# GpSimd for the context's elementwise work, dense copies of the scanned states, tables kept and re-read, and stores on another queue

## The chip, the core and the metric

One core of a Trainium2 chip runs the whole step of a hybrid S5 and pooling backbone in float32. The metric is the device time of one execution in microseconds (us); three executions of the kernel before took 2468.7, 2470.66 and 2472.08, the median is 2470.66.

## The reference, cut to what matters

A context of 128 tokens and a latent grid of 1024 tokens go through two layers. Layer 0 mixes with an S5 scan in both directions, layer 1 with pooling; each has a LayerNorm, a SwiGLU and another LayerNorm. The change lies in layer 0: the S5 mixer's output, its GLU, and the context's LayerNorm and SwiGLU.

```python
def s5_mixer(h, ..., h0_re, h0_im):
    u = h.reshape(bsz, seq_len, SSM_GROUPS, SSM_GROUP)
    y = u * d_skip
    for d in range(N_DIRS):
        s_re, s_im, f_re, f_im = s5_scan(u, ab_re, ab_im, bb_re, bb_im, h0_re[:, d], h0_im[:, d], reverse=(d == 1))
        y = y + einsum('blgp,ghp->blgh', s_re, c_re[d]) - einsum('blgp,ghp->blgh', s_im, c_im[d])
    v = gelu(y.reshape(bsz, seq_len, D_MODEL)) @ glu_w + glu_b
    val, gate = split(v, 2)
    return val * sigmoid(gate), ...

xc = layer_norm(DEEPNORM_ALPHA * xc + g1c * oc, ln_g[i, 0], ln_b[i, 0])
fc = swiglu(modulate(xc, sh2c, sc2c), ffn_w_gate[i], ffn_w_up[i], ffn_w_down[i])
xc = layer_norm(DEEPNORM_ALPHA * xc + g2c * fc, ln_g[i, 1], ln_b[i, 1])
```

`xl`, the latents, goes the same way with its own gates.

## The kernel before

Channels lie on partitions, 8 blocks (`kt`) of 128. For the scan, eight tokens in a row form a chunk: the latents have 128 chunks, the context 16. The work until the latents' GLU runs through these stages:

- *Tables.* `ssm_params`, then per block `ssm_u`, `ssm_in`, `ssm_tables`: the inputs u and the tables of each block are made. Output tables go to memory as `mo` (1 MB a block, stores `mo<-otab`) and `kd` (the part inside a chunk, read back as `mk`, 0.5 MB). Beside it the weights of the ada modulation are read, tile by tile (`adaw<-ada_w`, 0.5 MB), and used (`ada_steps`, L148). After the first bank 32 tiles remain: in the kernel before 16 of them are asked for by `self.step(fill, 2)` in this loop and 16 in the loop over the context's y.
- *Context's scan and y.* `ssm_scan_ctx` runs 15 steps; a step is six VectorE instructions (L477, L482) on the state buffers `Z` of both directions, which are 128 partitions x 145 chunks x 64 floats, so that the same state of the next chunk lies 64 floats on. `ssm_y_ctx` loads `mk` and `mo` of a block and multiplies (L620, L623), applies Gelu, transposes (L634).
- *Context's GLU, LayerNorm, SwiGLU up* (`ctx0a`, `ctx0b`: L815 with names glu and ffn) while the latents are scanned (`ssm_scan_lat`, 127 steps). All their elementwise work is on VectorE, in one queue with the scan.
- *Latents' y* (`ssm_y`, L649 and L652). `stack` first swaps halves of Z so that one product covers both real and imaginary parts; the products then read Z with its stride of 64 floats. Each block's result goes to memory (`yd`, eight stores on SP) and is read again by `yr<-yd` on GpSimd's queue.
- After that the latents' GLU begins (`glu` for A and B), with the rest of the context's SwiGLU as filling, and then the remaining layers.

Instructions of an engine run in program order; DMAs of a queue are issued in order. The scheduler of the tile framework decides the order on each engine from the code's order and its own timeline. Buffers decide when a load may start: `raw` has three (weights of 0.5 MB), `mk` and `mo` two each. In the orders below `Z_562` is the forward state buffer and `Z_566` the backward one; `mo_86` to `mo_93`, `kd_94` to `kd_101` and `yd_102` to `yd_109` are blocks 0 to 7.

Of the kernel before, what the change touches and what calls it, by code (L numbers as in the profile page):

```python
# [20 lines left out]
KT = 8  # L21
# [20 lines left out]
class Kernel:  # L42
# [540 lines left out]
    def load_mo(self, tmp, kt):  # L583

        m = tmp.tile([128, 8, 128], F32, tag="mk", name="mk", bufs=2)
        kd = self.kd[kt]
        for s in range(8):
            self.nc.sync.dma_start(m[16 * s:16 * s + 16], kd.rearrange("g h m -> h g m")[:, :, 16 * s:16 * s + 128])
        mo = tmp.tile([128, 2048], F32, tag="mo", name="mo", bufs=2)
        self.nc.sync.dma_start(mo, self.mo[kt])  # L590
        return m, mo.rearrange("p (d x g m) -> p d x g m", d=2, x=2, g=4)

    def stack(self, tmp, kt, c0, n, tag):


        nc = self.nc
        for d in range(2):
            z = self.Z[d][:, c0 + d:c0 + d + n, :].rearrange("p c (r g) -> p r g c", r=2)[:, :, 4 * kt:4 * kt + 4]
            t = tmp.tile([64, 4, n], F32, tag=tag, name=tag, bufs=2)
            if d == 0:  # L600
                cp = lambda o, i: nc.scalar.activation(o, i, AF.Copy)
            else:
                cp = lambda o, i: nc.vector.tensor_copy(o, i)
            cp(t, z[64:128, 0])
            cp(z[64:128, 0], z[0:64, 1])
            cp(z[0:64, 1], t)

    def ssm_y_ctx(self, tmp, kt):
# [29 lines left out]
    def ssm_y(self, tmp, kt):  # L638

        nc = self.nc  # L640
        m, ot = self.load_mo(tmp, kt)
        self.stack(tmp, kt, 0, NCL, "swl")
        y = tmp.tile([128, 8, NCL], F32, tag="yl", name="yl", bufs=2)
        py = [self.psum(f"py{x}") for x in range(2)]
        for gp in range(4):
# [4 lines left out]
            for x in range(2):  # L650
                for d in range(2):
                    nc.tensor.matmul(o[x], ot[:, d, x, gp, :], self.Z[d][:, d:d + NCL, 32 * x + 4 * kt + gp],  # L652
                                     start=False, stop=(d == 1))
# [3 lines left out]
        for t in range(8):  # L657
            nc.sync.dma_start(yd[t], y[16 * t:16 * t + 16])

# [3 lines left out]
    def ssm(self):  # L663
# [19 lines left out]
        with R("ssu") as tmp:  # L683
            for kt in range(KT):
                self.ssm_u(tmp, kt)
                if kt == 0:
                    self.ssm_u_ctx(tmp)
                self.step(fill, 2)
                self.ssm_powers(kt)
# [13 lines left out]
        with R("ssy") as tmp:  # L703
            self.adp = tmp
            self.yb = [tmp.tile([128, 8, 8, 16], F32, tag="yl", name=f"yb{q}", bufs=2) for q in range(2)]
            for q in range(2):
                self.nc.gpsimd.memset(self.yb[q], 0.0)
            for kt in range(KT):
                self.ssm_y_ctx(tmp, kt)
                self.step(fill, 2)  # L710
            self.step(fill, 2)
            self.ctx0a()
            self.ssm_scan_lat()
            self.adp = self.rawc = None
            for kt in range(KT):
                self.ssm_y(tmp, kt)
# [104 lines left out]
    def pair(self, b, w, x, name):  # L821
# [8 lines left out]
        return p1, p2  # L830

    def glu(self, b, x, fill=iter(()), vx=lambda a: a, vs=lambda a: a):
        nc, I = self.nc, self.I
        gw = I["ssm_glu_w"][0].rearrange("(k p) m -> p k m", p=128)
        for m in range(8):
# [3 lines left out]
            nc.scalar.activation(sg, pg, AF.Sigmoid, bias=self.glu_b[:, 1, m:m + 1])  # L839
            nc.vector.scalar_tensor_tensor(sg, pv, self.glu_b[:, 0, m:m + 1], sg, op0=OP.add, op1=OP.mult)  # L840
            nc.vector.scalar_tensor_tensor(vx(b.x[:, m, :]), vs(sg), self.gate[0, 0][:, b.i, m:m + 1],
                                           vx(b.x[:, m, :]), op0=OP.mult, op1=OP.add)
            next(fill, None)
# [57 lines left out]
    def ln_stats(self, b):  # L901

        nc = self.nc
        v = nc.vector
        n = b.n
# [24 lines left out]
        v.scalar_tensor_tensor(q, q, -0.5, r, op0=OP.mult, op1=OP.mult)  # L930
        v.scalar_tensor_tensor(r, q, 1.5, r, op0=OP.add, op1=OP.mult)
        for q in range(4):
# [160 lines left out]
    def build(self):  # L1093
        tc, nc = self.tc, self.nc
        with ExitStack() as st:
# [15 lines left out]
            self.XC = P("xcres").tile([128, 8, 128], F32, name="XC")  # L1111
            self.gate, self.lnm = {}, {}
            self.ident = self.cp.tile([128, 128], F32, name="ident")
            make_identity(nc, self.ident)
            self.ssm()
            fill = self.ctx0b()
            self.step(fill, 15)
            self.whl = P("whl")
            xr = P("xres")
# [140 lines left out]
```

## Time and profile before

| | us |
|---|---|
| median of three executions | 2470.66 |
| the profiled execution | 2463.38 |
| its span | 2461.6 |

| engine | busy us | share of the span |
|---|---|---|
| TensorE matmul (PE) | 2269.7 | 92% |
| TensorE weight load (PEld) | 1896.8 | 77% |
| VectorE (DVE) | 1267.1 | 51% |
| ScalarE (ACT) | 921.4 | 37% |
| GpSimd (POOL) | 168.2 | 7% |

The shares are means over the whole span. The change touches the first 515 us, so the rows below are of single stretches there. A row of instructions names the line, the engine, the operation, output<-inputs, shapes and count; busy time of a stretch is summed over an engine's instructions; PEclk is the granted clock of TensorE as a share of full speed, DMA share the mean busy share of the core's 16 DMA engines. "[x <-y]" is idle time of the engine ahead of the row and what ended it. SPq and POOLq rows are DMA issues. The trace has two records for each float32 matrix product with 128x128 operands. Matmul records overlap, so their pace is read from the starts, not from the durations.

### The profile page before, as it was taken

The numbers are of one execution on the slowest core, as the hardware profiler recorded it, in microseconds if no ns is written. First come the engines' busy times: TensorE is split into PE (matmuls) and PEld (weight loads), VectorE is DVE, ScalarE is ACT, GpSimd is POOL, SyncE is SP. The second block draws the span as 40 slices with busy tenths as digits, with TensorE's granted clock in tenths as the row PEclk, the third lists the DMA queues.
The fourth block names the chain that finished last, engine by engine and source line by source line (L and its number), as shares of the span: only waits on it lengthen the run. The fifth ranks groups of instructions, "written<-read, shape, count | busy, mean of one in ns | idle before, by whom it ended". The sixth has DMA issues, their size and how long they took to land.

```text
span 2461.6 us, 33280 instructions
## 1 busy us (share of the span) xinstructions
PE 2269.7 (92%) x13105; PEld 1896.8 (77%) x13105; DVE 1267.1 (51%) x2478; ACT 921.4 (37%) x1359; POOL 168.2 (7%) x182
## 2 busy tenths in 40 slices
PE   4877777689999999999999999889999999999997
PEld 2655677678887777788888888777788888888996
DVE  6789672053537222456422675778422455422476
ACT  3763126163216222443322453325322443322364
POOL 4920000000001000100000010002000100000000
PEclk7986898899999999999999999999999999999998
DMA  7759766684555554533333234865333223333453
GB/s 223 243 154 269 214 189 150 170 261 124 150 162 175 159 159 158 189 107 95 94 99 98 95 99 142 242 189 151 94 95 102 94 95 97 99 96 94 146 197 103
DMA packets 470076, 361.42 MB, mean 147 GB/s; under 512 B 15504, under 2 KB 418720, under 8 KB 467616
## 3 DMA queue, kind: packets, MB, share of 16 engines
q1 hardware_dynamic: 466032, 349.30, 48.0%
q10 hardware_dynamic: 2736, 5.80, 0.6%
q0 software_dynamic: 1152, 4.19, 0.5%
q8 instruction: 103, 1.69, 0.3%
q14 instruction: 53, 0.43, 0.1%
HBM read 340.77 MB, written 18.35 MB: 146 GB/s over the span
## 4 chain that ended last, share of the span: by engine, by line
PE 78%; DMA 12%; DVE 4%; ACT 3%; SPq 1%; POOL 1%; issue 1%; ACTq 0%; DVEq 0%; POOLq 0%
PE ffn L811 13%; PE ffn L813 13%; PE ffn L812 13%; PE dn L812 6%; PE dn L811 6%; PE dn L813 6%; PE ffn L815 3%; PE dn L815 3%; DMA adaw<-ada_w 3%; PE glu L811 2%; PE glu L813 2%; PE glu L812 2%; DMA raw<-ffn_w_up 2%; PE py L652 2%; DMA raw<-ffn_w_down 1%; DMA mo<-mo 1%
## 5 line engine op out<-in xcount | busy, mean ns | idle before, releaser
L795 ACT ACTIVATE wh<-raw 128x1024 fp32r<-128x1024 f32 (+1 forms) x326 | 341.7, 1049 | 944.0 <-PE ffn L812 613.9
L796 DVE TENSOR_TENSOR wl<-raw,wh 128x1024 fp32r<-128x1024 f32 (+1 forms) x326 | 394.6, 1211 | 496.0 <-ACT wh L795 489.0
L812 PE MATMUL dn<-hkl,wh 128*128 128x512 f32 (+1 forms) x880 | 304.5, 348 | 0.3 <-DVE hkl L796 0.3
L813 PE MATMUL dn<-hkh,wl 128*128 128x512 f32 (+1 forms) x880 | 303.0, 347 | 0.0
L811 PE MATMUL ffn<-xp,wh 128*128 128x512 f32 x704 | 275.9, 392 | 2.2 <-ACT wh L795 2.2
L813 PE MATMUL ffn<-xp,wl 128*128 128x512 f32 x704 | 276.1, 392 | 0.5 <-DVE wl L796 0.5
L811 PE MATMUL ffn<-xm,wh 128*128 128x512 f32 x704 | 274.4, 391 | 1.3 <-ACT xm L795 0.7
L812 PE MATMUL ffn<-xp,wh 128*128 128x512 f32 x704 | 275.4, 391 | 0.0
L813 PE MATMUL ffn<-xm,wl 128*128 128x512 f32 x704 | 274.9, 391 | 0.0
L812 PE MATMUL ffn<-xm,wh 128*128 128x512 f32 x704 | 274.8, 390 | 0.0
L811 PE MATMUL dn<-hkh,wh 128*128 128x512 f32 (+1 forms) x880 | 262.5, 348 | 0.9 <-ACT hkh L795 0.9
L856 DVE TENSOR_TENSOR h<-ffn,sg 128x512 f32<-128x512 f32 x88 | 60.6, 689 | 248.9 <-PE ffn L813 248.2
L812 PEld LDWEIGHTS dn<-hkl,wh 128*128 128x128 f32 x880 | 166.6, 189 | 21.0 <-DVE hkl L796 0.5
L813 PEld LDWEIGHTS dn<-hkh,wl 128*128 128x128 f32 x880 | 166.5, 189 | 20.5
L811 PEld LDWEIGHTS dn<-hkh,wh 128*128 128x128 f32 x880 | 163.3, 189 | 23.4 <-ACT hkh L795 1.7
L815 PE MATMUL ffn<-xmc,raw 128*128 128x128 f32 x1184 | 148.1, 282 | 30.3 <-DMA raw<-ffn_w_up 12.3
L815 PEld LDWEIGHTS ffn<-xmc,raw 128*128 128x128 f32 x1184 | 141.0, 195 | 40.2 <-DMA raw<-ffn_w_up 16.4
L811 PEld LDWEIGHTS ffn<-xm,wh 128*128 128x128 f32 x704 | 132.1, 188 | 33.2 <-issue 3.8
L811 PEld LDWEIGHTS ffn<-xp,wh 128*128 128x128 f32 x704 | 133.1, 189 | 31.0 <-ACT wh L795 2.5
L813 PEld LDWEIGHTS ffn<-xp,wl 128*128 128x128 f32 x704 | 132.8, 189 | 28.9 <-DVE wl L796 1.0
L812 PEld LDWEIGHTS ffn<-xp,wh 128*128 128x128 f32 x704 | 132.8, 189 | 28.5 <-issue 0.7
L813 PEld LDWEIGHTS ffn<-xm,wl 128*128 128x128 f32 x704 | 132.2, 188 | 29.0 <-issue 1.5
(313 smaller groups left out, 3238.6 us busy)
## 6 DMA issues: line engine op xcount, KB each, us to landing
raw<-ffn_w_down SPq DMA_DIRECT2D x126, 512.0 KB
raw<-ffn_w_gate SPq DMA_DIRECT2D x125, 512.0 KB
raw<-ffn_w_up SPq DMA_DIRECT2D x125, 512.0 KB
adaw<-ada_w SPq DMA_DIRECT2D x96, 512.0 KB
raw<-ssm_glu_w SPq DMA_DIRECT2D x48, 512.0 KB
mo<-mo SPq DMA_DIRECT2D x16, 1024.0 KB
rc<-ffn_w_down SPq DMA_DIRECT2D x40, 256.0 KB
mo<-otab SPq DMA_DIRECT2D x32, 256.0 KB
```

The source lines that it names most:

```text
L652: nc.tensor.matmul(o[x], ot[:, d, x, gp, :], self.Z[d][:, d:d + NCL, 32 * x + 4 * kt + gp], start=False, stop=(d == 1))
L795: nc.scalar.activation(h, src, AF.Copy)
L796: nc.vector.tensor_tensor(l, src, h.bitcast(F32), op=OP.subtract)
L811: nc.tensor.matmul(ps, wh, xh, start=start, stop=False)
L812: nc.tensor.matmul(ps, wh, xl, start=False, stop=False)
L813: nc.tensor.matmul(ps, wl, xh, start=False, stop=stop)
L815: nc.tensor.matmul(ps, w[0], x[0], start=start, stop=stop)
L856: nc.vector.tensor_tensor(h[:, f, :], pu, sg, op=OP.mult)
```

## The change

Five things change.

1. Ada's weight tiles are asked for earlier: three per block from block 3 on in the table loop, three ahead of the context's y, one in each of its blocks.
2. `load_mo` keeps what is loaded: four `mk` and two `mo` buffers, and the latents' blocks go in the order 6, 7, 4, 5, 0, 1, 2, 3, so that blocks 6 and 7 need no load and 4 and 5 only `mo`.
3. For the latents `stack` is replaced by `stack_dense`: a copy of the block's states with chunks next to each other (three buffers), on ScalarE, VectorE and GpSimd; the products read the copy. For the context `stack`'s copies of the second direction move from VectorE to GpSimd.
4. While `scanning` holds, the context's elementwise work (GLU, LayerNorm, the first six blocks of SwiGLU) goes to GpSimd. ScalarE copies from PSUM what GpSimd needs, and an instruction with two operations becomes two. The reciprocal stays on VectorE.
5. The eight stores of a block's y are issued by GpSimd instead of SP.

```diff
     def load_mo(self, tmp, kt):
-        m = tmp.tile([128, 8, 128], F32, tag="mk", name="mk", bufs=2)
-        kd = self.kd[kt]
-        for s in range(8):
-            self.nc.sync.dma_start(m[16 * s:16 * s + 16], kd.rearrange("g h m -> h g m")[:, :, 16 * s:16 * s + 128])
-        mo = tmp.tile([128, 2048], F32, tag="mo", name="mo", bufs=2)
-        self.nc.sync.dma_start(mo, self.mo[kt])
-        return m, mo.rearrange("p (d x g m) -> p d x g m", d=2, x=2, g=4)
+        if kt not in self.mks[-4:]:
+            m = tmp.tile([128, 8, 128], F32, tag="mk", name="mk", bufs=4)
+            for s in range(8):
+                self.nc.sync.dma_start(m[16 * s:16 * s + 16],
+                                       self.kd[kt].rearrange("g h m -> h g m")[:, :, 16 * s:16 * s + 128])
+            self.mks.append(kt)
+            self.held["m", kt] = m
+        if kt not in self.mos[-2:]:
+            mo = tmp.tile([128, 2048], F32, tag="mo", name="mo", bufs=2)
+            self.nc.sync.dma_start(mo, self.mo[kt])
+            self.mos.append(kt)
+            self.held["o", kt] = mo
...
     def stack(self, tmp, kt, c0, n, tag):
...
-                cp = lambda o, i: nc.vector.tensor_copy(o, i)
+                cp = lambda o, i: nc.gpsimd.tensor_copy(o, i)
...
+    def stack_dense(self, tmp, kt, d):
+        nc = self.nc
+        z = self.Z[d][:, d:d + NCL, :].rearrange("p c (r g) -> p r g c", r=2)[:, :, 4 * kt:4 * kt + 4]
+        sd = tmp.tile([128, 2, 4, NCL], F32, tag="sd", name="sd", bufs=3)
+        for x in range(2):
+            for r in range(2):
+                o, i = sd[64 * r:64 * r + 64, x], z[64 * x:64 * x + 64, r]
+                if d == 0 and x == 0:
+                    nc.scalar.activation(o, i, AF.Copy)
+                elif x == 1 and r == 0:
+                    nc.gpsimd.tensor_copy(o, i)
+                else:
+                    nc.vector.tensor_copy(o, i)
+        return sd
...
     def ssm_y(self, tmp, kt):
-        self.stack(tmp, kt, 0, NCL, "swl")
+        sd = [self.stack_dense(tmp, kt, d) for d in range(2)]
...
-                    nc.tensor.matmul(o[x], ot[:, d, x, gp, :], self.Z[d][:, d:d + NCL, 32 * x + 4 * kt + gp],
+                    nc.tensor.matmul(o[x], ot[:, d, x, gp, :], sd[d][:, x, gp, :],
...
-            nc.sync.dma_start(yd[t], y[16 * t:16 * t + 16])
+            nc.gpsimd.dma_start(yd[t], y[16 * t:16 * t + 16])
...
     def ssm(self):
-                self.step(fill, 2)
+                self.step(fill, 2 if kt < 3 else 3)
...
+            self.scanning = True
+            self.step(fill, 3)
             for kt in range(KT):
                 self.ssm_y_ctx(tmp, kt)
-                self.step(fill, 2)
-            self.step(fill, 2)
+                self.step(fill, 1)
+            self.drain(fill)
             self.ctx0a()
             self.ssm_scan_lat()
-            for kt in range(KT):
+            for kt in (6, 7, 4, 5, 0, 1, 2, 3):
                 self.ssm_y(tmp, kt)
...
+    def elem(self, b, early=True):
+        return self.nc.gpsimd if self.scanning and early and not b.split else self.nc.vector
+
+    def in_sb(self, b, v, ps):
+        if v is self.nc.vector:
+            return ps
+        t = b.tmp.tile([128, b.n], F32, tag="lq" + b.tg, name="cp", bufs=1)
+        self.nc.scalar.activation(t, ps, AF.Copy)
+        return t
+
+    def stt(self, b, out, x, s, y, op0, op1, bias=None):
+        v = self.elem(b)
+        if v is self.nc.vector:
+            v.scalar_tensor_tensor(out, x, s, y, op0=op0, op1=op1)
+            return
+        t = b.tmp.tile([128, 2, b.n], F32, tag="lt" + b.tg, name="st", bufs=3)[:, 0]
...
+        if bias is not None:
+            self.nc.scalar.activation(t, x, AF.Identity, bias=bias)
+        else:
+            v.tensor_scalar(t, x, s, None, op0=op0)
+        v.tensor_tensor(out, t, y, op=op1)
...
     def ffn_up(self, b, l, x, h, first=None):
-            nc.vector.tensor_tensor(h[:, f, :], pu, sg, op=OP.mult)
+            v = self.elem(b, f < 6)
+            v.tensor_tensor(h[:, f, :], self.in_sb(b, v, pu), sg, op=OP.mult)
...
     def ln_stats(self, b):
-        v = nc.vector
+        v = self.elem(b)
...
-        pm = self.ones_mm(b, t[:, 0], "lnm")
+        pm = self.in_sb(b, v, self.ones_mm(b, t[:, 0], "lnm"))
...
-        v.reciprocal(r, q)
-        v.scalar_tensor_tensor(q, pv, LN_EPS / (ALPHA * ALPHA), r, op0=OP.add, op1=OP.mult)
+        nc.vector.reciprocal(r, q)
+        self.stt(b, q, pv, LN_EPS / (ALPHA * ALPHA), r, OP.add, OP.mult, self.epsc[:, 0:1])
```

The two instructions of `glu` and the two that follow in `ln_stats` go through `stt` in the same way; in `build`, `self.scanning = False` follows `self.step(fill, 15)`.

On TensorE, where the latents' y begins, the order before was this (glu and ffn are the context's products, lnm and lnv its LayerNorm sums, py the latents' y):

```order
L815 MATMUL glu<-xmc,raw 128x128 x88
L898 MATMUL lnm<-lt,ones 128x128
L898 MATMUL lnv<-sq,ones 128x128
L815 MATMUL ffn<-xmc,raw 128x128 x192
L652 MATMUL py_3938<-Z_562,mo 128x128
L815 MATMUL ffn<-xmc,raw 128x128 x8
L652 MATMUL py_3938<-Z_566,mo 128x128
L652 MATMUL py_3939<-Z_562,mo 128x128
```

Now it is this:

```order
L841 MATMUL glu<-xmc,raw 128x128 x104
L952 MATMUL lnm<-lt,ones 128x128
L952 MATMUL lnv<-sq,ones 128x128
L841 MATMUL ffn<-xmc,raw 128x128 x135
L677 MATMUL py_3969<-sd,mo 128x128
L841 MATMUL ffn<-xmc,raw 128x128
L677 MATMUL py_3970<-sd,mo 128x128
L841 MATMUL ffn<-xmc,raw 128x128 x16
L677 MATMUL py_3969<-sd,mo 128x128
```

135 of the context's 240 SwiGLU products of this part stand ahead of the first y product instead of 192; 105 stand between y products.

On SP's queue at the same place, where the tables of the third and fourth block of y are asked for, the order before was this:

```order
L588 DMA mk<-kd_96 16x8x128 x5
L658 DMA yd_102<-yl 16x8x128 x8
L588 DMA mk<-kd_96 16x8x128 x2
L658 DMA yd_103<-yl 16x8x128 x8
L588 DMA mk<-kd_96 16x8x128
L590 DMA mo<-mo_88 128x2048
L588 DMA mk<-kd_97 16x8x128 x8
L590 DMA mo<-mo_89 128x2048
```

Now it is this:

```order
L589 DMA mk<-kd_94 16x8x128 x2
L595 DMA mo<-mo_90 128x2048
L589 DMA mk<-kd_94 16x8x128 x6
L830 DMA raw<-ffn_w_gate 128x8x128
L589 DMA mk<-kd_95 16x8x128 x2
L595 DMA mo<-mo_91 128x2048
L589 DMA mk<-kd_95 16x8x128 x6
L830 DMA raw<-ffn_w_up 128x8x128
```

No store of y stands between loads any more.

On GpSimd's queue the context's work is followed by copies (sd) and the stores of y, which did not stand there before:

```order
L988 TENSOR_TENSOR XC<-XC,lr 128x256 x4
L1003 TENSOR_SCALAR xmc<-XC,lnm_2900 128x128 x8
L910 TENSOR_TENSOR hc<-cp,sg 128x128 x6
L628 COPY sd<-Z_562 64x512
L628 COPY sd<-Z_566 64x512
L628 COPY sd<-Z_562 64x512
L628 COPY sd<-Z_566 64x512
L628 COPY sd<-Z_562 64x512
L683 DMA yd_108<-yl 16x8x128 x8
L628 COPY sd<-Z_566 64x512
L628 COPY sd<-Z_562 64x512
L683 DMA yd_109<-yl 16x8x128 x8
```

Five copies stand ahead of the first store, and between the stores of one block and of the next two copies for later blocks.

## Rows read from the trace of the kernel before

**Rows 1.** Stretches: length, busy us of each engine, PEclk, DMA share, GB/s.
```profile
0.00:165.00 165.00, 122.57 (x1350) 80.87 (x1351) 125.38 (x299) 102.98 (x209) 104.24 (x92) 0.90 0.70 209
165.00:258.00 93.00, 66.41 (x683) 48.60 (x680) 74.09 (x449) 29.85 (x101) 1.84 (x2) 0.61 0.90 250
...
311.00:369.60 58.60, 49.29 (x385) 46.88 (x386) 44.87 (x252) 12.74 (x24) 3.91 (x7) 0.95 0.70 200
369.60:481.30 111.70, 84.82 (x474) 80.62 (x473) 18.31 (x24) 42.32 (x45) 0.00 (x0) 0.85 0.64 155
481.30:515.00 33.70, 21.57 (x135) 18.43 (x134) 11.41 (x12) 21.97 (x30) 2.84 (x5) 0.90 0.99 297
515.00:2461.60 1946.60, 1891.73 (x9831) 1590.89 (x9829) 949.00 (x1203) 702.96 (x934) 53.19 (x75) 0.99 0.43 131
```

**Rows 2.** Groups of VectorE, 236 to 400 us: busy, mean ns, idle ahead, releaser.
```profile
L603 DVE COPY Z<-swl 64x512 f32<-64x512 f32 x8 | 7.1, 883 | 0.2
...
L856 DVE TENSOR_TENSOR hc<-ffn,sg 128x128 f32<-128x128 f32 x13 | 3.8, 292 | 15.6 <-ACT sg L855 15.5
L840 DVE SCALAR_TENSOR_TENSOR sg<-glu,vv,sg 128x128 f32<-128x128 f32 x8 | 2.8, 351 | 25.0 <-ACT sg L839 25.0
```

**Rows 3.** Tile adaw, 44 to 165 us: idle time ahead (us, times).
```profile
DMA adaw<-ada_w: 15.1, 20
```

**Rows 4.** Groups, 165 to 258 us: ada's products.
```profile
L148 PE MATMUL ada<-adaw,cond 128*32 128x256 f32 x112 | 14.1, 588 | 10.8 <-DMA adaw<-ada_w 10.8
```

**Rows 5.** Timeline of TensorE, one block of the context's y: start, us, instruction.
```profile
224.31 3.09 PE L634 MATMUL pyt<-i,yb 128*128 128x16 f32 x16 [1.27 <-ACT yb L630]
...
233.06 1.18 PE L634 MATMUL pyt<-i,yb 128*128 128x16 f32 x9 [1.08 <-ACT yb L630]
```

**Rows 6.** Timeline of TensorE about the context's LayerNorm.
```profile
295.78 1.06 PE L815 MATMUL glu<-xmc,raw 128*128 128x128 f32 x8
...
310.78 6.97 PE L815 MATMUL ffn<-xmc,raw 128*128 128x128 f32 x48 [5.64 <-POOL xmc L949]
```

**Rows 7.** Timeline of TensorE in the latents' y.
```profile
468.13 0.62 PE L649 MATMUL py<-u,mk 128*128 128x128 f32 x4
468.59 1.92 PE L652 MATMUL py<-Z,mo 128*128 128x128 f32 x8
470.33 0.62 PE L649 MATMUL py<-u,mk 128*128 128x128 f32 x4
```

**Rows 8.** Timeline of SP's queue in the latents' y.
```profile
424.12 3.63 SPq L658 DMA_DIRECT2D yd<-yl  x8
...
428.33 0.38 SPq L590 DMA_DIRECT2D mo<-mo  x1
```

**Rows 9.** Groups of GpSimd, whole span.
```profile
L946 POOL TENSOR_SCALAR lx<-X,lnm 128x512 f32<-128x512 f32 x32 | 42.0, 1316 | 844.3 <-DVE h L856 480.2 <-DVE X L841 210.7 <-DVE X L934 111.8
...
L949 POOL TENSOR_SCALAR xmc<-XC,lnm 128x128 f32<-128x128 f32 x16 | 12.8, 815 | 141.3 <-DVE XC L934 141.3
L1131 POOL DMA_DIRECT2D yr<-yd x8 | 4.4, 553 | 206.0 <-DMA yd<-yl 173.4 <-DVE xn L796 32.6
```

**Rows 10.** Timeline of GpSimd in the table stage.
```profile
28.20 1.27 POOL L78 TENSOR_TENSOR otab<-oc,oc 128x512 f32<-128x512 f32 x1
...
40.94 2.13 POOL L82 TENSOR_TENSOR otab<-oc,oc 128x512 f32<-128x512 f32 x1
```

**Rows 11.** Timeline of VectorE in the scan.
```profile
311.90 0.50 DVE L477 TENSOR_TENSOR stt<-rm,Z 128x128 f32<-128x128 f32 x2
...
313.07 0.50 DVE L477 TENSOR_TENSOR stt<-rm,Z 128x128 f32<-128x128 f32 x2
...
315.31 0.48 DVE L477 TENSOR_TENSOR stt<-rm,Z 128x128 f32<-128x128 f32 x2
...
316.26 0.48 DVE L477 TENSOR_TENSOR stt<-rm,Z 128x128 f32<-128x128 f32 x2
```

**Rows 12.** Timeline of GpSimd in the scan.
```profile
308.83 6.09 POOL L949 TENSOR_SCALAR xmc<-XC,lnm 128x128 f32<-128x128 f32 x8 [135.74 <-DVE XC L934]
```

More of the change, by code (lines that the diff above doesn't have):

```diff
@@ L583, in load_mo @@
     def load_mo(self, tmp, kt):
-        m = tmp.tile([128, 8, 128], F32, tag="mk", name="mk", bufs=2)
-        kd = self.kd[kt]
-        for s in range(8):
-            self.nc.sync.dma_start(m[16 * s:16 * s + 16], kd.rearrange("g h m -> h g m")[:, :, 16 * s:16 * s + 128])
-        mo = tmp.tile([128, 2048], F32, tag="mo", name="mo", bufs=2)
-        self.nc.sync.dma_start(mo, self.mo[kt])
-        return m, mo.rearrange("p (d x g m) -> p d x g m", d=2, x=2, g=4)
+        if kt not in self.mks[-4:]:
[10 more added lines that the diff above has]
+            self.held["o", kt] = mo
+        return (self.held["m", kt],
+                self.held["o", kt].rearrange("p (d x g m) -> p d x g m", d=2, x=2, g=4))
     def stack(self, tmp, kt, c0, n, tag):
@@ L703, in ssm @@
         with R("ssy") as tmp:
-            self.adp = tmp
+            self.mks, self.mos, self.held = [], [], {}
+            self.scanning = True
             self.yb = [tmp.tile([128, 8, 8, 16], F32, tag="yl", name=f"yb{q}", bufs=2) for q in range(2)]
@@ L707, in ssm @@
                 self.nc.gpsimd.memset(self.yb[q], 0.0)
+            self.step(fill, 3)
             for kt in range(KT):
                 self.ssm_y_ctx(tmp, kt)
-                self.step(fill, 2)
-            self.step(fill, 2)
+                self.step(fill, 1)
+            self.drain(fill)
             self.ctx0a()
             self.ssm_scan_lat()
-            self.adp = self.rawc = None
-            for kt in range(KT):
+            for kt in (6, 7, 4, 5, 0, 1, 2, 3):
                 self.ssm_y(tmp, kt)
@@ L830, in pair @@
         return p1, p2
+    def elem(self, b, early=True):
[12 more added lines that the diff above has]
+        t = b.tmp.tile([128, 2, b.n], F32, tag="lt" + b.tg, name="st", bufs=3)[:, 0]
+        if len(x.shape) == 3:
+            t = t.rearrange("p (t c) -> p t c", t=x.shape[1])
+        if bias is not None:
[3 more added lines that the diff above has]
+        v.tensor_tensor(out, t, y, op=op1)
     def glu(self, b, x, fill=iter(()), vx=lambda a: a, vs=lambda a: a):
@@ L839, in glu @@
             nc.scalar.activation(sg, pg, AF.Sigmoid, bias=self.glu_b[:, 1, m:m + 1])
-            nc.vector.scalar_tensor_tensor(sg, pv, self.glu_b[:, 0, m:m + 1], sg, op0=OP.add, op1=OP.mult)
-            nc.vector.scalar_tensor_tensor(vx(b.x[:, m, :]), vs(sg), self.gate[0, 0][:, b.i, m:m + 1],
-                                           vx(b.x[:, m, :]), op0=OP.mult, op1=OP.add)
+            self.stt(b, sg, pv, self.glu_b[:, 0, m:m + 1], sg, OP.add, OP.mult, self.glu_b[:, 0, m:m + 1])
+            self.stt(b, vx(b.x[:, m, :]), vs(sg), self.gate[0, 0][:, b.i, m:m + 1], vx(b.x[:, m, :]),
+                     OP.mult, OP.add)
             next(fill, None)
@@ L927, in ln_stats @@
         nc.scalar.activation(q, pv, AF.Sqrt, bias=self.eps if b.split else self.epsc[:, 0:1])
-        v.reciprocal(r, q)
-        v.scalar_tensor_tensor(q, pv, LN_EPS / (ALPHA * ALPHA), r, op0=OP.add, op1=OP.mult)
-        v.scalar_tensor_tensor(q, q, -0.5, r, op0=OP.mult, op1=OP.mult)
-        v.scalar_tensor_tensor(r, q, 1.5, r, op0=OP.add, op1=OP.mult)
+        nc.vector.reciprocal(r, q)
+        self.stt(b, q, pv, LN_EPS / (ALPHA * ALPHA), r, OP.add, OP.mult, self.epsc[:, 0:1])
+        self.stt(b, q, q, -0.5, r, OP.mult, OP.mult)
+        self.stt(b, r, q, 1.5, r, OP.add, OP.mult)
         for q in range(4):
@@ L1112, in build @@
             self.gate, self.lnm = {}, {}
+            self.scanning = False
             self.ident = self.cp.tile([128, 128], F32, name="ident")
@@ L1117, in build @@
             self.step(fill, 15)
+            self.scanning = False
             self.whl = P("whl")
```

## The prediction

> **What bounds the kernel now.** I read the table of stretches first [rows 1], then what the VectorE waits for [rows 2], then single stretches of TensorE and of the SP queue. From 515 us to the end TensorE is busy 97% of the time and the change leaves that code alone, so everything is decided before 515 us. There five stages follow each other, and no engine is full in all of them:
>
> - Tables, 0 to 165 us: DMA share 0.70. The ada tiles that this stage loads in its second half make TensorE wait 15.1 us [rows 3].
> - Context's y, 165 to 258 us: DMA share 0.90 at 250 GB/s and a granted clock of 0.61 [rows 1]. Here ada's products take 14.1 us of TensorE and wait 10.8 us for their tiles [rows 4]; a block goes round in 8.75 us (224.31 to 233.06) [rows 5], with one of the 14 ada groups of eight records in it (14.1/14 = 1.0 us).
> - Context's GLU and LayerNorm, 258 to 311 us. The LayerNorm is the hole of some 14 us between the last GLU product (295.78 + 1.06 = 296.8 us) and the first FFN product at 310.78 us, which itself waits 5.64 us for GpSimd's xmc [rows 6].
> - Context's FFN beside the scan, 311 to 369.6 us: 385 records in 58.6 us [rows 1], that is 12 blocks of 32 records, 4.9 us each. The scan ends late because VectorE stands in its own queue behind elementwise work of the context: 25.0 us before the GLU's products and 15.6 us before the FFN's [rows 2].
> - The latents' y, 369.6 to 481.3 us: 111.7 us with a DMA share of only 0.64 [rows 1]. Two things make it long. Products that read the states with their stride start every 0.218 us (eight in 1.74 us), those that read dense u every 0.115 us (four in 0.46 us) [rows 7]. And the next table, mo, is issued at 428.33 us, only after the eight stores of y that begin at 424.12 us on the same SP queue [rows 8].
>
> Then 34 us follow (481.3 to 515) in which x, y and weights arrive at DMA share 0.99.
>
> **The change part by part**, against the profiled execution (2463.4 us, its span 2461.6; the median of the runs is 7.3 us above).
>
> (a) *More ada tiles in the table stage.* The new order of SP has all 32 tiles of the two later banks ahead of the first mk load; 16 more fall into this stage, and 15 now follow its last x tile, where two did. At the price of the rows they cost 15.1 us again; at no price, if the idle 30% of the DMA (49 us) takes their 8.4 MB; at worst their whole transfer, 28 us at 299 GB/s (209/0.70). Taken: +12, nearest to the row, with a little for cover.
>
> (b) *Context's y without ada, and without the first two tables of the latents.* 93 us were some 12 of start and 81 for eight blocks. A block without ada is 8.75 - 1.0 = 7.7 us, so 62: -19. The DMA floor is 14.1 MB (8 mk, 8 mo, three GLU tiles) at 278 GB/s, 51 us: -30 at best; the waits alone removed, -11.
>
> (c) *GLU:* from 258 to 296.8 it took 39 us; two ada groups and the waits for VectorE go, 36 are left: -3 (-6 to +3). GpSimd's three instructions per block (0.82 us each, rows 9) hide under 4 us of products.
>
> (d) *LayerNorm on GpSimd.* From the last GLU product to the first FFN product the chain has 11 instructions of 128 elements and 13 of 256. The row gives 0.82 us for 128 and 1.32 for 512 elements [rows 9], so 0.98 for 256: 9.0 + 12.7 = 21.8 us. TensorE's two sums, ScalarE's copies, root and table load, the reciprocal and some fifteen handovers add 8: 30 us for 14, +16. Below: +7, if handovers are free. Above: +30, if every instruction is stretched as the same dense sum is in the table stage while VectorE works, from 1.27 to 2.13 us [rows 10].
>
> (e) *The FFN ahead of y.* In the order 12 blocks stood ahead of the first y product, now 135 products, 8.4 blocks: 3.6 x 4.9 = -18. They come back in (f). The scan no longer waits in this order except for the reciprocal and two late FFN blocks. Alone it goes at 0.945 us a step (315.31 to 316.26), beside GpSimd 1.17 (311.90 to 313.07) [rows 11, 12]. It starts at 165 + 12 + 15 context steps (14) and 3 of start, 194 us; 127 x 0.945 = 120, and 24% of some 50 us of GpSimd work (24 GLU instructions, 22 us of LayerNorm, 8 of xmc, 6 of FFN) are 12. The reciprocal stands after 86 steps, reached near 283; its input is there half a LayerNorm after the GLU's end (296.8 + 12 - 19 - 3 = 287), near 301: 18. So the scan ends at 344 us, ahead of TensorE's queue, which reaches y at 369.6 + 12 - 19 - 3 + 16 - 18 = 358 us. The wait for the scan is costed at nothing; its cover is 14 us.
>
> (f) *The latents' y.* Dense copies make 256 records start every 0.115 instead of 0.218 us: 26 us of TensorE, from 70 to 44. The 6.6 FFN blocks add 210 records, about 26 us: 70 at best. DMA: 17.3 MB, less two mk (1 MB), plus 3.6 MB of FFN, 20 MB at 242 GB/s (155/0.64): 83 us. The SP queue now has loads only; a table waits for its buffer, not for a store. For one block GpSimd has two copies (1.3 us each by the 512-element row) and eight stores (0.55 us each if they cost what the y loads cost, rows 9), 7 us, against 11 us for a block. The dense copies have three buffers, two per block, so the second copy of a block starts only when the block before ends: about 1 us a block. 83 + 8 = 91, from 112: -21. Bounds: TensorE alone, 70, -42; the queues as slow as now plus the FFN blocks, +18.
>
> The Trainium skill (SBUF — State Buffer, Who interferes with whom) says that a VectorE instruction with two SBUF inputs and a GpSimd instruction that reads SBUF exclude each other, the second waiting out the first. By that rule the 50 us of GpSimd work would be added to the scan whole, and (e) would lose its cover. The rows agree with a slowdown and not with a full stop (1.17 for 0.945), for one-input instructions only; no run here shows two-input ones beside the scan.
>
> (g) *The end.* Stores end the GpSimd queue and y's loads stand behind them: 4.4 us for the last eight, 3.6 on SP now. Against that x and the GLU's weights are issued with the last two blocks, not behind 16 stores. -5 (-12 to +8).
>
> Sum: 12 - 19 - 3 + 16 - 18 - 21 - 5 = -38. 2463.4 becomes 2425, the median 2470.7 becomes 2432.5.
>
> **The rivals** (times as medians).
>
> R1, *the scan takes over.* If GpSimd stops the scan fully, it ends at 194 + 120 + 50 = 364 us, and with 6 us of waiting for the reciprocal, reached later, at 370, 12 us after TensorE is ready: 2444. For it: two-input instructions on both sides. Against it: the 24% of the rows.
>
> R2, *the stores on GpSimd become the bound (the slower side).* The 64 stores and 15 copies stand in one in-order queue, and copies for the next block stand behind stores of the last. With p for a store, the stage takes 64p + 20 us, which decides from p = 1.1 and makes the whole slower from p = 1.7 (64p + 20 above 91 + 38). If each store waits for one VectorE copy (0.88 us, rows 2), p is 0.55 + 0.88 = 1.43: 112 us, 2453. At 2.13 us, the stretched sum of rows 10, 156 us: 2498. Against it: 0.55 us for a load with as many rows (128 of 4 KB) as a store has runs (128 of 512 bytes).
>
> The Trainium skill (SBUF — State Buffer, section "SBUF: two separate sides") speaks against this edit: descriptors of a GpSimd DMA starve while VectorE copies fp32 between SBUF tiles, 620 ns becoming 3100. With 3.1 us for every store the stage would take 218 us by an estimate from that page. No run here shows a GpSimd DMA beside such copies, and VectorE copies only a third of the time.
>
> R3, *given back ahead:* (a) at 28 and (d) at +30: 16 + 14 = 30 more on the sum, 2462. For it: both depend on stretches that TensorE awaits in order.
>
> R4, *queues couple better:* y at 75 us, context's y 7 us shorter, the end at -10: 16 + 7 + 5 = 28 less, 2404. For it: the DMA share of 0.64; against it, the mixed small packets (full-share rate 242 there, 278 and more elsewhere).
>
> **How the numbers follow.** Forecast 0.52, R1 0.14, R2 0.11, R3 0.10, R4 0.13. Measurement can tell 0.2%, about 5 us, from no change. Faster: 0.52 + 0.14 + 0.13, 0.03 of R2 and 0.05 of R3, 0.87; same 0.04 (0.01 and 0.03); slower 0.09 (0.07 and 0.02). The forecast's own range is 2414 to 2450. The range of 8 in 10 reaches down to R4 and a little past R3: 2403 to 2467.
>
> **What would show it.** Right: products on the dense states start every 0.115 us; no yd store on SP, and mo issued within a microsecond or two of the end of the block whose buffer it takes; VectorE waits for the context only at the reciprocal and the two FFN blocks; y begins near 358 us and lasts about 90, while its first table needs no load. Wrong: a LayerNorm hole over 40 us; scan steps of 1.4 us or more; GpSimd busy all through y with TensorE waiting for sd; the table stage past 190 us; a time above 2467 or below 2403.

## The result, and the profile after

The changed kernel takes 2441.43 us (median of four, 2435.49 to 2444.74) beside 2469.68 us: ratio 0.9882, 95% interval 0.9861 to 0.9904, 28 us faster. The forecast was 2432.5 us, with a range of 2403 to 2467. A second measurement, among the experiments, gave 0.9899 (0.9880 to 0.9918).

The profiled execution has a span of 2433.7 us, 27.9 less than before. Cut at the same events of TensorE's timeline:

| stage, until | before | after | difference | forecast |
|---|---|---|---|---|
| tables, last product | 167.4 | 178.2 | +10.8 | +12 |
| context's y, last transpose | 90.8 | 84.0 | -6.8 | -19 |
| context's GLU | 38.6 | 35.6 | -3.0 | -3 |
| context's LayerNorm, first FFN product | 14.0 | 21.1 | +7.1 | +16 |
| FFN ahead of y | 58.8 | 41.0 | -17.8 | -18 |
| latents' y | 111.9 | 90.4 | -21.5 | -21 |
| x, first GLU product of the latents | 22.6 | 30.3 | +7.7 | } -5 |
| the rest | 1957.5 | 1953.1 | -4.4 | } |

These are two single executions. A second profile of the changed kernel (c1_after below; the slowest of its ten executions, as the first is the fastest) has 181.1, 86.6, 36.6, 21.1, 43.8, 90.5, 30.7 and 1959.6 us in the same rows. So a stage repeats within some 3 us and the last row only within 6: the -4.4 there is no finding.

Stretches of the changed kernel, with the columns of [rows 1] (length; busy us of TensorE, its weight loads, VectorE, ScalarE, GpSimd; granted clock, DMA share, GB/s):

```profile
178.20:262.20 84.00, 54.02 (x544) 44.48 (x545) 80.12 (x494) 28.76 (x98) 10.44 (x26) 0.59 0.63 170
297.80:318.90 21.10, 1.62 (x5) 1.04 (x5) 7.78 (x25) 4.53 (x11) 15.70 (x26) 0.62 0.16 46
359.90:450.30 90.40, 76.11 (x602) 73.61 (x600) 37.17 (x44) 41.07 (x49) 54.34 (x71) 0.92 0.82 231
450.30:480.60 30.30, 12.53 (x73) 11.05 (x73) 7.65 (x7) 16.83 (x25) 6.37 (x12) 0.72 0.91 279
```

The y stage is shorter although it does 212 records of SwiGLU inside, where 98 stood; its DMA share rose from 0.64 to 0.82. TensorE's groups in it (busy, mean ns, idle ahead and releaser) answer to [rows 7]:

```profile
L677 PE MATMUL py<-sd,mo 128*128 128x128 f32 x256 | 44.0, 294 | 13.0 <-DMA mo<-mo 7.2 <-DVE sd L630 5.7
L841 PE MATMUL ffn<-xmc,raw 128*128 128x128 f32 x212 | 28.2, 287 | 0.9 <-DMA raw<-ffn_w_gate 0.9
```

Those 256 records were 61.8 us busy before. Where the clock is full, four of them start in 0.45 us (434.65 to 435.10), one every 0.11 us, where the strided ones started every 0.218 [rows 7]:

```profile
434.65 0.61 PE L677 MATMUL py<-sd,mo 128*128 128x128 f32 x4
435.10 0.39 PE L674 MATMUL py<-u,mk 128*128 128x128 f32 x2
```

TensorE waits 14 us in the stage where it waited 27: 7.2 us for tables (15.5 before, beside 11.4 for which the trace shows no releaser) and 5.7 us for the dense copies, which is new. On SP no store stands between loads now (answers to [rows 8]):

```profile
389.07 0.33 SPq L589 DMA_DIRECT2D mk<-kd  x1
389.52 0.36 SPq L595 DMA_DIRECT2D mo<-mo  x1
389.93 4.82 SPq L589 DMA_DIRECT2D mk<-kd  x7
398.10 0.39 SPq L830 DMA_DIRECT2D raw<-ffn_w_gate  x1
```

VectorE's waits from 178 to 365 us (who waits, for what: us in total, times, longest) answer to [rows 2]: the 25.0 and 15.6 us are gone, and the scan stands 27.0 us at the reciprocal instead.

```profile
DVE lr L982 <- ACT lq L981: 27.0, 1, 27.0
DVE hc L910 <- ACT sg L908: 3.2, 2, 3.0
```

### The profile page after: what moved, and what is told of

It reads as the page before. It is cut to its first block, busy times and chain, and to the rows that moved or that the text cites. A ratio compares the mean times of both kernels' runs of the same rounds, so it can differ in the third digit from the quotient of the medians.

```text
span 2433.7 us, 33343 instructions
## 1 busy us (share of the span) xinstructions
PE 2243.9 (92%) x13105; PEld 1874.0 (77%) x13105; DVE 1274.6 (52%) x2421; ACT 926.1 (38%) x1377; POOL 267.2 (11%) x337
## 4 chain that ended last, share of the span: by engine, by line
PE 79%; DMA 13%; DVE 3%; issue 2%; ACT 2%; POOL 1%; SPq 1%; ACTq 0%; DVEq 0%; POOLq 0%
PE ffn L837 13%; PE ffn L839 13%; PE ffn L838 13%; PE dn L838 6%; PE dn L837 6%; PE dn L839 6%; PE ffn L841 3%; PE dn L841 3%; DMA adaw<-ada_w 2%; PE glu L838 2%; PE glu L839 2%; PE glu L837 2%; DMA raw<-ffn_w_gate 2%; DMA raw<-ffn_w_down 1%; DMA raw<-ssm_glu_w 1%
## 5 line engine op out<-in xcount | busy, mean ns | idle before, releaser
L839 PEld LDWEIGHTS dn<-hkh,wl 128*128 128x128 f32 x880 | 166.5, 189 | 20.5
L841 PEld LDWEIGHTS ffn<-xmc,raw 128*128 128x128 f32 x1184 | 141.9, 196 | 40.3 <-DMA raw<-ffn_w_up 11.1
```

What stands on the lines that cost most here:

```text
L839: nc.tensor.matmul(ps, wl, xh, start=False, stop=stop)
L841: nc.tensor.matmul(ps, w[0], x[0], start=start, stop=stop)
```

## The experiments

Milestones and stage lengths without a fence are read from TensorE's timeline of each kernel, at the same events as in the table above where nothing else is said. Ratios are to the kernel before, measured beside each kernel on the same chip; "changed kernel" stands for the second measurement. First one part undone at a time, then one part alone, then the disputed waits.

**The changed kernel again** (c1_after).

> The changed kernel itself again, beside the others of this study. Both theories: 2436 to 2447 us, ratio 0.985 to 0.992 to the kernel before.

Measured: 2442.67 us, 0.9899 (0.9880 to 0.9918).

**Ada's tiles as before** (u1_ada).

```diff
-                self.step(fill, 2 if kt < 3 else 3)
+                self.step(fill, 2)
...
-            self.step(fill, 3)
...
-                self.step(fill, 1)
+                self.step(fill, 2)
```

> Ada's weight tiles asked for as before (two per block of the tables, two per block of the context's y), all else as changed. Theory: the earlier ada is worth nothing, since the table stage got 10.8 us longer (last table product 167.4 to 178.2 us) and the context's y only 6.8 us shorter (90.8 to 84.0) with the GLU 3 us: undoing it gives -5 to +3 us against the changed kernel, 2436 to 2444, with the tables ending near 167 again and the context's y back over 90 us. Rival, the terms of the forecast (12 against 19 and 3): undoing it costs 8 to 10 us, 2449 or more.

Measured: 2427.81 us, 0.9842 (0.9823 to 0.9860): 15 us faster than the changed kernel, more than either theory said. So this part of the change is a loss. The context's y, from the last table product to the last transpose, with ada's products in it again, and below it TensorE's group of those products there:

```profile
172.30:255.60 83.30, 55.08 (x640) 40.58 (x643) 69.20 (x420) 28.65 (x99) 10.15 (x26) 0.61 0.87 246
```
```profile
L148 PE MATMUL ada<-adaw,cond 128*32 128x256 f32 x124 | 13.3, 538 | 10.5 <-DMA adaw<-ada_w 10.5
```

83.3 us with 13.3 us of ada's products and 10.5 us of waits for their tiles, 84.0 without: they lie in time in which TensorE would wait for other things. In the tables they do not. The second half of that stage, of the kernel before and of the changed one:

```profile
100.00:167.40 67.40, 61.30 (x736) 43.94 (x732) 56.66 (x117) 56.75 (x118) 38.14 (x34) 1.00 0.52 158
```
```profile
100.00:178.20 78.20, 72.28 (x851) 47.26 (x849) 59.64 (x126) 58.27 (x119) 37.77 (x33) 1.00 0.72 231
```

It gets 10.8 us longer and TensorE is 11.0 us busier: a stretch where TensorE is 91% busy was given 115 more records. The other kernels agree: in the six profiles with ada's tiles as before the tables end between 167.4 and 173.6 us, in the eight with the earlier ones between 178.2 and 183.7. Against the profile of the changed kernel taken beside it, the tables are 8.8 us shorter (172.3 against 181.1), the way from the first FFN product to the end of y 12.2 us (122.1 against 134.3), the GLU 5.5 us longer. Why the second of these is shorter was not separated. Both kernels do some 480 records of SwiGLU up to the end of y, but here 272 of them stand inside y instead of 210, and TensorE waits there 7.2 us for tables and copies instead of 13.6; that the filling covers these waits is likely and not shown.

**Strided products instead of dense copies** (u3_stride).

```diff
-                cp = lambda o, i: nc.gpsimd.tensor_copy(o, i)
+                cp = lambda o, i: (nc.gpsimd if tag == "swc" else nc.vector).tensor_copy(o, i)
...
-        sd = [self.stack_dense(tmp, kt, d) for d in range(2)]
+        self.stack(tmp, kt, 0, NCL, "swl")
...
-                    nc.tensor.matmul(o[x], ot[:, d, x, gp, :], sd[d][:, x, gp, :],
+                    nc.tensor.matmul(o[x], ot[:, d, x, gp, :], self.Z[d][:, d:d + NCL, 32 * x + 4 * kt + gp],
```

> The latents' y with strided reads of the states and the swap of halves as before, instead of the dense copies; all else as changed. Theory: TensorE is the fullest engine of that stage (76 of 90 us); 256 records at 0.218 instead of 0.115 us add 26 us, of which the 5.7 us of waits for the copies and part of the 7.2 us for mo come back: 12 to 24 us slower than the changed kernel, 2453 to 2465. Rival, that the stage is set by its transfers (DMA share 0.82) and the gain came from the stores' queue: within 5 us of the changed kernel.

Measured: 2448.65 us, 0.9923 (0.9908 to 0.9938), 6 us slower, though the intervals overlap a little. Between the two theories. The order on TensorE changed with the edit: the last product of y comes at 441.0 us, 78.6 us after the first, and much of the SwiGLU that stood between y products now follows them. Up to the latents' x products, which is about the same work as in the changed kernel's y stage (586 records, 602 there), it is 97.5 us instead of 90.4, but TensorE is busy for 93.9 of them and waits for neither tables nor copies.

```profile
362.50:460.00 97.50, 93.90 (x586) 89.80 (x584) 22.89 (x35) 45.96 (x51) 34.55 (x60) 1.00 0.69 198
```

**Elementwise work on VectorE** (u4_elem).

```diff
-        return self.nc.gpsimd if self.scanning and early and not b.split else self.nc.vector
+        return self.nc.vector
```

> The context's elementwise work on VectorE again, all else as changed. In the order 231 of the context's SwiGLU products stand ahead of the first y product instead of 135. Theory: the scan waits again for the context (25 and 15 us before), six blocks of SwiGLU more at 4.9 us stand ahead of y (+29), the LayerNorm hole is 14 us instead of 21 (-7), and the y stage gets back the six blocks' 192 records (22 us of TensorE, of which 8 to 15 show): 7 to 15 us slower than the changed kernel, 2448 to 2456. Rival, that the slower LayerNorm on GpSimd eats the whole gain: within 4 us of it, or faster.

Measured: 2448.57 us, 0.9919 (0.9904 to 0.9933), 6 us slower, again with intervals that overlap. The LayerNorm's hole is 13.8 us, the FFN ahead of y 69.5, y 76.6: from the first FFN product to the end of y 15 us more than in the first profile of the changed kernel and 12 more than in the second, of which the LayerNorm gives back 7.

**Tables as before** (u2_tables).

```diff
-        if kt not in self.mks[-4:]:
-            m = tmp.tile([128, 8, 128], F32, tag="mk", name="mk", bufs=4)
+        if True:
+            m = tmp.tile([128, 8, 128], F32, tag="mk", name="mk", bufs=2)
...
-        if kt not in self.mos[-2:]:
+        if True:
...
-            for kt in (6, 7, 4, 5, 0, 1, 2, 3):
+            for kt in range(KT):
```

> The tables as before: two mk and two mo buffers, every table loaded again for the latents, blocks in the order 0 to 7; all else as changed (2442.7 us in this study). Theory: 4 MB more have to come, some 16 us of transfer at the 242 GB/s of a full share, part of it hidden in the GLU; the context's y goes back towards the 90.8 us of before: 6 to 15 us slower than the changed kernel, 2449 to 2458. Rival, that the idle share (0.61 in the context's y, 0.83 in the latents') hides it: within 5 us.

Measured: 2447.10 us, 0.9903 (0.9881 to 0.9925): no difference that can be told. In the profile y is 99.4 us instead of 90.4 and waits 11.1 us for mo, but the context's y is 80.4 instead of 84.0.

**Stores back on SP** (u5_store).

```diff
-            nc.gpsimd.dma_start(yd[t], y[16 * t:16 * t + 16])
+            nc.sync.dma_start(yd[t], y[16 * t:16 * t + 16])
```

> The stores of y on SP's queue as before, all else as changed. Theory: eight stores of a block again stand ahead of the next tables, TensorE's waits for mo (7.5 us) grow, the y stage gets 5 to 10 us longer: 2448 to 2453. Rival (the slower side of the forecast in small): on GpSimd the stores hold back the dense copies, TensorE's 6 us of waits for sd go, and it is up to 5 us faster than the changed kernel: 2437 to 2442.

Measured: 2442.42 us, 0.9892 (0.9870 to 0.9913): no difference. Here too the order on TensorE changed: y lasts 74.4 us with 84 SwiGLU records in it instead of some 210, and the latents' GLU begins 53.4 us behind it instead of 30.3; so this is not the stores' queue alone. By the ratios, undoing four parts one by one costs about 6, 5, 1 and -2 us, of which the last two are no difference, and undoing the fifth gains 14; together they bring 25 to 28. So the parts stand in for each other, and three of them were run alone.

**Dense copies alone, on the kernel before** (b3_dense): `stack_dense` and the products on it as in the change, nothing else.

```diff
-        self.stack(tmp, kt, 0, NCL, "swl")
+        sd = [self.stack_dense(tmp, kt, d) for d in range(2)]
...
-                    nc.tensor.matmul(o[x], ot[:, d, x, gp, :], self.Z[d][:, d:d + NCL, 32 * x + 4 * kt + gp],
+                    nc.tensor.matmul(o[x], ot[:, d, x, gp, :], sd[d][:, x, gp, :],
```

> The kernel before with one part of the change alone: dense copies of the states for the latents' y (three buffers), products that read them. First theory, two limits in the y stage: TensorE gets 26 us shorter, but the 15.5 us of waits for mk and mo behind the stores on SP stay and grow, and waits for the copies come: 3 to 12 us faster than before, 2456 to 2465. Second theory: TensorE is the one limit, and most of the 26 us show: 2441 to 2450.

Measured: 2440.74 us, 0.9876 (0.9856 to 0.9897). My first theory fell: this part alone brings as much as the whole change. The second gave nearly this time, but TensorE's work is not the one limit, as its waits in the y stage show:

```profile
376.90:459.30 82.40, 63.11 (x475) 61.23 (x475) 33.04 (x34) 28.20 (x37) 21.88 (x15) 0.88 0.81 210
```
```profile
PE py L669 <- DMA mo<-mo: 12.1, 5, 2.9
PE py L666 <- DMA mk<-kd: 6.7, 4, 2.7
```

TensorE's busy time fell from 84.8 [rows 1] to 63.1, and its waits did not grow: 18.8 us for tables, where before it waited 27 (mk 8.0, mo 7.5, and 11.4 for which the trace shows no releaser).

**Stores on GpSimd alone, on the kernel before** (b5_store).

```diff
-            nc.sync.dma_start(yd[t], y[16 * t:16 * t + 16])
+            nc.gpsimd.dma_start(yd[t], y[16 * t:16 * t + 16])
```

> The kernel before with one part of the change alone: the eight stores of a block's y on GpSimd's queue. First theory, two limits: the 15.5 us of waits for mk and mo in the y stage (111.9 us, TensorE busy 85) fall below 8, TensorE's own time is then the limit: 5 to 13 us faster than before, 2455 to 2463. Second theory, as putting them back on SP changed nothing in the changed kernel: within 4 us of before.

Measured: 2446.96 us, 0.9910 (0.9894 to 0.9926), 23 us faster; more than the first theory. The y stage, then TensorE's only wait in it:

```profile
370.80:452.40 81.60, 80.90 (x480) 77.58 (x479) 19.00 (x25) 45.36 (x48) 33.00 (x56) 1.00 0.74 212
```
```profile
PE py L652 <- DMA mo<-mo: 0.7, 1, 0.7
```

All 27 us of waiting went, and TensorE's work fills the stage. Without the waits its granted clock there is 1.00 instead of 0.85 [rows 1], and its work takes 80.9 us instead of 84.8. Part of the gain was given back: TensorE then waited 17.8 us for rc (weights of the context's later SwiGLU). So before, y was TensorE's own work (85 us, 61.8 of them strided products) plus 27 us of waiting that the stores on SP caused; either edit takes about 30 us from it. The whole change does not bring the sum of 30 and 23 us; its other parts put 114 more records of SwiGLU, with their weights, into the same stage. The two without the rest were not run, so how far they add up is open.

**Elementwise work on GpSimd alone** (p4_only): `elem`, `in_sb` and `stt` as in the change, on the kernel before; with them `self.drain(fill)` behind the context's y.

```diff
-            nc.vector.tensor_tensor(h[:, f, :], pu, sg, op=OP.mult)
+            v = self.elem(b, f < 6)
+            v.tensor_tensor(h[:, f, :], self.in_sb(b, v, pu), sg, op=OP.mult)
...
-        v = nc.vector
+        v = self.elem(b)
...
```

> The kernel before with one part of the change alone: the context's elementwise work on GpSimd while the latents are scanned. In the order 104 of the context's SwiGLU products stand ahead of y, where 192 did. First theory: y starts 15 to 20 us earlier (5.5 blocks of 4.9 us less, LayerNorm 7 to 9 us longer), but the stage then takes these blocks in, beside stores and strided reads as before, 10 to 20 us: 0 to 10 us faster than before, 2458 to 2468. Second theory: y has room for them (TensorE waited 27 us there), and the whole is 12 to 18 us faster: 2450 to 2456.

Measured: 2470.24 us, 1.0002 (0.9989 to 1.0015): nothing, the lower edge of the first theory. y starts at 356.4 instead of 369.6 us and is still 110.8 us long; SwiGLU products run behind it and the latents' GLU starts at 519.4 instead of 504.1, with more of the filling done. What it moves ahead comes back as long as the y stage is slow.

**Reciprocal left out** (x_recipcp).

```diff
-        nc.vector.reciprocal(r, q)
+        (v.tensor_copy(r, q) if v is nc.gpsimd else v.reciprocal(r, q))
```

> As the changed kernel, but the LayerNorm's reciprocal of the context is left out: GpSimd copies in its place, so that VectorE, which stood 27 to 30 us in the scan waiting for that reciprocal's input, has nothing of the LayerNorm in its queue. First theory: the end of the scan (361 us) sets where y starts (360 us); it ends some 25 us earlier, y starts 10 to 25 us earlier and the whole is 5 to 15 us faster than the changed kernel, 2428 to 2438. Second theory: SwiGLU and y together are set by TensorE and the transfers, y starts earlier but ends as late: 2439 to 2446.

Measured: 2446.05 us, 0.9906 (0.9884 to 0.9928), no difference, and it tells nothing: the wait moved to the next instruction of the context in VectorE's queue, 27.5 us at hc, and the scan's last instruction started at 368.6 us.

**Nothing of the context in the scan's queue** (x_allpool): the edit above, and

```diff
-            v = self.elem(b, f < 6)
+            v = self.elem(b, f < 10)
```

> As the changed kernel, but VectorE has nothing of the context in its queue while it scans: ten blocks of the SwiGLU's elementwise work on GpSimd instead of six, and the LayerNorm's reciprocal left out (GpSimd copies in its place). The scan then ends 20 to 30 us earlier than the 361 to 370 us of the changed kernel. First theory, that TensorE's order sets where y starts (128 products of the SwiGLU ahead of it): y starts less than 5 us earlier, and the time is that of the changed kernel, 2438 to 2447. Second theory, that the scan's end sets it: y starts 10 us or more earlier and the whole is 5 us or more faster.

Measured: 2442.87 us, 0.9888 (0.9872 to 0.9905). The scan's last instruction now starts at 338.8 instead of 361.1 us, VectorE then waits for TensorE, and y starts 39.2 us after the first FFN product instead of 41.0 (43.8 in the second profile). TensorE's order sets where y starts, not the scan.

```profile
DVE sd L630 <- PE py L677: 28.6, 1, 28.6
```

**Ada as before, and the late SwiGLU's weights on GpSimd's queue** (v_rcq): the edit of u1_ada, and

```diff
-            nc.sync.dma_start(t[:, 0:c, :], src[:, 4 * q:4 * q + c, :])
+            nc.gpsimd.dma_start(t[:, 0:c, :], src[:, 4 * q:4 * q + c, :])
```

> Ada's tiles asked for as before (that kernel measured 2427.8 us), and the weights of the context's later SwiGLU (rc) on GpSimd's queue instead of SP's. Theory: TensorE's 13.1 us of waiting for rc after the x products come from SP's queue, where x and five GLU weights stand ahead of rc; they fall below 4 us, and the latents' GLU begins 5 to 10 us earlier: 2418 to 2424. Rival: that stretch has a DMA share of 0.94, so the same bytes take the same time and another wait takes its place: 2425 to 2431.

Measured: 2421.91 us, 0.9809 (0.9784 to 0.9834), the fastest of all, faster than the changed kernel; against u1_ada's 0.9842 (0.9823 to 0.9860) the intervals touch, so that step of 6 to 8 us is likely and not shown. In the profiles the latents' GLU begins 21.2 us after y instead of 28.6. TensorE's wait for rc (12.8 us in the changed kernel, the first row) goes; the other theory's new wait is there too, but shorter in effect (second row, from 442.9 to 480 us):

```profile
PE ffn L841 <- DMA rc<-ffn_w_gate: 12.8, 1, 12.8
```
```profile
PE glu L836 <- ACT xm L820: 11.8, 2, 9.7
```

## Why the prediction was right or wrong

The time lay in the range, 9 us above the forecast (-28 for -38), and of the mechanisms the one given most of the chance came nearest: the stretches of (e) and (f) got shorter as forecast. That the sum came so near is partly luck: (b) and (g) fell short by 12 and 8 us, and (d) cost 9 us less. And the forecast counted ada's move, the main cause of (a) to (c), as a gain of 10 us, where u1_ada shows a loss of 15. By its steps:

(a) +12, measured +10.8, for another reason. I priced the tiles by their waits; those grew only from 15.1 [rows 3] to 19.7 us. TensorE's own products were the price, and [rows 1] showed the stage as a whole with 123 of 165 us busy, which hid that its second half was nearly full.

(b) -19, measured -6.8: the step that failed. "81 for eight blocks" and "8.75 - 1.0" do not go together: eight rounds of 8.75 are 70 us, so 11 of the 19 us came from taking one round's pace for the average. The way to the first transpose did not shrink (21.4 before, 23.7 us now, with waits of 2.4 us for mo, 3.6 for the swap on GpSimd and 3.3 for Gelu). The seven rounds after it went from 67.4 to 56.7 us (201.91 to 258.60), one of them with a wait of 4.6 us for a GLU weight behind the tables on SP. Their pace went with TensorE's granted clock: the three other rounds with the transposes at half clock (0.50 from 210.30 to 213.70 us) took 8.2 to 8.4 us, the three at full clock (1.00 from 239.50 to 241.30) 6.1 to 6.6. It had fallen to half while TensorE waited 10 us for the context's scan (178.2 to 188.2). Transposes at either level:

```profile
210.21 3.60 PE L659 MATMUL pyt<-i,yb 128*128 128x16 f32 x16 [1.28 <-ACT yb L655]
246.04 1.96 PE L659 MATMUL pyt<-i,yb 128*128 128x16 f32 x16 [0.99 <-ACT yb L655]
```

u1_ada shows that ada's removal is worth nothing here: with ada in the rounds they take 62.2 us, but the way to the first transpose only 19.1. What shortened this stage by 7 us with ada in or out is not settled: p4_only (91.6 us) speaks against the elementwise work, u2_tables (80.4) against the four mk buffers; the swap on GpSimd is left, alone or together with another part, and was not tried alone.

(c) -3, as forecast.

(d) +16, measured +7.1, the bottom of its bounds (where 21.8 us for 14 makes +7.8, not +7). The durations of [rows 9] were too long for this work:

```profile
300.88 0.72 POOL L963 TENSOR_TENSOR lt<-lt,XC 128x256 f32<-128x256 f32 x1
302.48 0.45 POOL L965 TENSOR_TENSOR lt<-lt 128x128 f32<-128x128 f32 x1
318.17 4.64 POOL L1003 TENSOR_SCALAR xmc<-XC,lnm 128x128 f32<-128x128 f32 x8
```

0.45 and 0.58 us for 128 elements instead of 0.82, 0.72 us for 256 instead of 0.98. While the reciprocal is waited for, the scan stands still and GpSimd has little beside it.

(e) -18, measured -17.8, but its cover of 14 us was not there: the scan stood 27.0 us at the reciprocal, not 18, and its last instruction started at 361.1 us, 1.2 us after the first product of y. x_allpool shows that this cost nothing.

(f) -21, measured -21.5. TensorE 76 us busy (70 forecast), waits of 7.2 us for mo and 5.7 us for copies (8 forecast). The agreement is partly luck: the term took 83 us from transfers at 242 GB/s for a full DMA share, but the stage moved 231 GB/s at a share of 0.82, 282 for a full share, so transfers did not set its length; 76 us of TensorE's work and 14 of waits did. What the term did not say is that dense copies alone would have brought as much.

(g) -5, measured +7.7, and -4.4 behind it (+2.1 in the second profile). I moved the stores and the x loads past each other and did not look at what follows them: five GLU weights ahead of rc on SP, and 12.8 us of TensorE. v_rcq shows that another queue takes this wait away.

Of the rivals, R2 fell: GpSimd's stores in the y stage cost nearly what the loads of [rows 9] cost.

```profile
L683 POOL DMA_DIRECT2D yd<-yl x61 | 35.5, 589 | 7.8 <-ACT yl L680 6.9 <-DMA yd<-yl 0.9
```

The 3.1 us that the Trainium skill (SBUF — State Buffer, "SBUF: two separate sides") gives for a GpSimd DMA beside an fp32 copy of VectorE did not appear, but a smaller price did. Of the 64 store issues the 17 that ran beside a VectorE copy took 0.62 to 1.10 us, the other 47 took 0.53. So the first three of the seven begun at 379.56 us (4.27 us together) took 0.74, 0.79 and 0.68 us, beside VectorE's copies of 376.68 to 381.62 us. VectorE's copies, and an issue beside them and one behind them:

```profile
376.68 4.94 DVE L630 COPY sd<-Z 64x512 f32<-64x512 f32 x4 [2.58 <-PE py L677]
379.56 0.74 POOL L683 DMA_DIRECT2D yd<-yl  x1
381.74 0.53 POOL L683 DMA_DIRECT2D yd<-yl  x1
```

R1's rule held in part, and R1 still did not come. By the rule (the same page, "Who interferes with whom") a VectorE instruction with two inputs waits out a GpSimd instruction that reads SBUF. The trace agrees for GpSimd instructions with two inputs. Four of them, from 315.34 to 318.17 us, each held one scan instruction up: it ended 0.08 to 0.15 us behind the GpSimd instruction beside which it had started, and four scan instructions took 2.24 us that take 0.62 without GpSimd. The scan step there took 2.82 us (314.67 to 317.49), past the 1.4 us that the prediction names as a sign of being wrong. Beside a one-input instruction the trace does not agree: during the eight xmc of 318.17 us a step took 1.15 us (319.11 to 320.26), slowed from 0.95 and not shut out. VectorE, then GpSimd:

```profile
315.33 2.24 DVE L482 TENSOR_TENSOR Z<-stt,Z 128x64 f32<-128x64 f32 x4
317.49 1.03 DVE L477 TENSOR_TENSOR stt<-rm,Z 128x128 f32<-128x128 f32 x2
318.44 0.74 DVE L482 TENSOR_TENSOR Z<-stt,Z 128x64 f32<-128x64 f32 x4
319.11 0.57 DVE L477 TENSOR_TENSOR stt<-rm,Z 128x128 f32<-128x128 f32 x2
...
341.70 0.48 DVE L477 TENSOR_TENSOR stt<-rm,Z 128x128 f32<-128x128 f32 x2
342.11 0.62 DVE L482 TENSOR_TENSOR Z<-stt,Z 128x64 f32<-128x64 f32 x4
342.65 0.48 DVE L477 TENSOR_TENSOR stt<-rm,Z 128x128 f32<-128x128 f32 x2
```
```profile
315.34 2.83 POOL L988 TENSOR_TENSOR XC<-XC,lr 128x256 f32<-128x256 f32 x4
318.17 4.64 POOL L1003 TENSOR_SCALAR xmc<-XC,lnm 128x128 f32<-128x128 f32 x8
```

What R1 had wrong is how much of GpSimd's work meets the scan. Of 44 us of it between 194.8 and 361.3 us, 14 lay in the 27.0 us in which the scan waited for the reciprocal anyway, and of the other 30 only 12 were two-input instructions. Of the scan's 166.5 us, 120 are its steps at 0.945 us, 30 its waits and some 3 other instructions of VectorE; about 13, an estimate from these rows, are left for GpSimd, where the prediction had 12. And in x_allpool a scan that ends 22 us earlier hardly lets y start earlier.

R3 and R4 did not come: neither (a) nor (d) reached its upper bound, and y took 90.4 us, not 75, with 7.2 us of waits for tables left in it.

## What to carry to other kernels

A stage that is busy time plus waits can be cut from either side, and each cut alone may look like the whole gain; price parts alone as well as together before adding them. Work taken out of a stage in which its engine waits can be worth nothing there, and the same work put into a stage where the engine is nearly full cost its whole duration here: read the busy share of the very stretch, not of the stage. Where an in-order queue is freed of one instruction that waits, look at the next one of the same kind behind it, and where stores leave a queue, at what the loads now stand in front of.

## What the hardware showed that I had not expected

GpSimd's two-input fp32 instructions took 0.45 us for 128x128 and 0.72 us for 128x256, less than the one-input row of [rows 9] (0.82 us for 128x128); but the same one-input instruction took 0.58 us in the changed kernel. No instruction of the latents' scan took over 0.38 us in the kernel before; in the changed one the longest took 0.83 us, beside a GpSimd instruction with two inputs. There a store issue on GpSimd was longer only while VectorE copied: 0.62 to 1.10 us instead of 0.53. And the executions spread more than the three shown of before: 2460 to 2479 us for that kernel over this study.
